# A two-layer decoder trunk on one core: more raw weight buffers, sums in smaller parts, sums of h on another queue, out projections by two row blocks

## The chip, the cores and the metric

One NeuronCore of a Trainium2 chip runs the program. Its engines work side by side: TensorE (PE; its weight loads are shown as PEld), VectorE (DVE), ScalarE (ACT), GpSimd (POOL) and SyncE (SP), which only issues transfers. Each engine runs its own instructions strictly in order; an instruction that waits holds all that stand behind it. Transfers are issued by SP, by ScalarE or by GpSimd, and all of them run on the same 16 DMA engines. The metric is the device time of one execution in microseconds, the median of three runs.

## The reference

Two decoder layers on x of shape (1, 512, 1024) in float32, each closed by a LayerNorm over `alpha * x + sublayer(x)`.

- The even (first) layer has one input projection of 1024 x 6144. Its columns feed chunkwise retention (8 heads with rotary q and k, a GroupNorm per head) and an RG-LRU branch (a causal convolution of width 4, block-diagonal gates, a scan). Both are multiplied by a SiLU gate path, concatenated, and mapped back by an output projection of 2048 x 1024.
- The odd (second) layer is differential attention: an input projection of 1024 x 8192 gives q and k for 16 maps of width 128, and v and the gate g of width 2048. A head subtracts lambda times its second softmax map from its first one, multiplies by v (width 256), normalises, and is gated by silu(g). An output projection of 2048 x 1024 follows.

```
q, k, v, g = split(x @ w_in)
w = softmax(q1 k1) - lam * softmax(q2 k2)
out = rmsnorm(w @ v) * subln_g * (1 - lambda_init) * silu(g)
y = out @ w_out;   x = layer_norm(alpha * x + y)
```

## The kernel before

**Products.** Every float32 matrix is held as a pair of rounded parts, high and low (`split`, L142: ScalarE makes the high part, VectorE the low one from the difference). A product is three matmuls (`mm3`, L151, shown as lines L152 to L154). S = 512 rows are four row blocks of 128; D = 1024 is eight tiles of 128.

**Weights.** They come in pieces of 128 x 1024 (512 KB), named w0 to w161 in the order of their use. `fetch` (L166) loads one piece into a raw buffer from SP (L174) and splits it into a pair (L148 and L149, or L145 and L146 where a scale goes in). The pool `wraw` has two raw buffers, `wsp` five split pairs. `take(ahead)` hands out the next piece and makes sure that `ahead` further ones have been fetched, as far as the program's order goes.

**Units.** `t_unit` uses a piece up in 24 matmuls (one head's 128 columns of q, k or a gate, for all 512 rows). `s_unit` makes 512 columns for four row blocks from four pieces. `out_unit` adds an output projection to the running sum y: with four pieces it goes through the row blocks one at a time, and for each through both 512-wide halves, first with pieces 0 and 1 and then with 2 and 3; its results lie in two PSUM banks of the pool `ps_pj` (four banks).

**`gates_values`** (L738) makes, for the second to fourth pair of heads of the second layer, the gate and v with seven block products instead of eight. For it sums of weight blocks and sums of blocks of h are needed:

- `weight_sums` (L382) makes 24 sums of weight blocks in HBM while the first layer runs: SP copies one block to the place t, and GpSimd issues a transfer that adds the second block to it. `SUM_GAP` = 18 is the number of steps between two sums.
- `act_sums` makes four sums of h once and stores them in HBM (sd). `load_sum` (L734) brings one of them into half of the tile sx (two transfers of 512 KB). `swap_in` loads two of them from SP. Inside `gates_values` two more calls stand between the products, issued by ScalarE; each overwrites what an earlier product has read, so it waits for TensorE.

sx and y lie in one place: y is put off to HBM (`store_y`, yd) ahead of `swap_in`, and fetched again at each out projection. A product of `gates_values` uses two pieces, 12 matmuls each.

**Order.** The order on TensorE and SP is the program's own. `Side` lays side work between the products: each `tick` (one step, after three matmuls) runs at most one due job. Jobs are the heads' retention, RG-LRU, the attention blocks (`attention`, L621: two score maps, Exp on ScalarE (L634), the combination on VectorE, transposes, the product with v), the LayerNorms and the sums. `need` runs a job until it is done. ScalarE, VectorE and GpSimd are put in order by the framework's scheduler at build time, by priorities and estimated times; after that their order is fixed.

**Memory.** The pools `es`, `qkp` and `two` belong to the first layer and are closed behind it (L612). `sp` (tiles for split scores), `gp` (five gates) and the small parameter tiles in `const` live through both layers.

Of the kernel before, what the change touches and what calls it, by code (L numbers as in the profile page):

```python
# [8 lines left out]
F32 = mybir.dt.float32  # L9
# [32 lines left out]
WARM_UP = 7  # L42
EARLY = 2

SUM_START, SUM_GAP = 40, 18


class Side:
# [49 lines left out]
def trunk(ctx: ExitStack, tc: tile.TileContext, a):  # L98
# [3 lines left out]
    def pool(name, bufs, stack=ctx, **kw):  # L102
        return stack.enter_context(tc.tile_pool(name=name, bufs=bufs, **kw))

    const = pool("const", 1)
    big = pool("big", 1)
    wraw = pool("wraw", 2)
    wsp = pool("wsp", 5)
    vp = pool("vp", 4)
    mixp = pool("mixp", 3)  # L110
    sp = pool("sp", 1)
    wk = pool("wk", 4)
    gp = pool("gp", 5)
# [16 lines left out]
    def bank(pl, tag, name):  # L130
        return pl.tile([P, 512], F32, tag=tag, name=name)

    def pair(pl, shape, tag, name, **kw):
        return tuple(pl.tile(shape, F32R, tag=tag + x, name=name + x, **kw) for x in "hl")

    def part(n, name):
        return pair(sp, [P, n], f"s{n}", name, bufs=2 if n == S else 1)

    def cut(t, *ix):
        return t[0][ix], t[1][ix]  # L140
# [25 lines left out]
    def fetch(parts=((0, D),)):  # L166
        if len(ready) < len(order):
            n = len(ready)
            src, scale = order[n]
            raw = wraw.tile([P, D], F32, tag="raw", name=f"w{n}_r")  # L170
            w = pair(extra.pop(n, wsp), [P, D], "w", f"w{n}")
            for lo, hi in parts:
                c = slice(lo, hi)
                nc.sync.dma_start(out=raw[:, c], in_=src[:, c])  # L174
                split(raw[:, c], cut(w, ALL, c), scale=scale)
                yield
            ready.append(w)
# [44 lines left out]
    def out_unit(mix, y, name, first, before=None, after=None, late=0):  # L222
        n = len(mix)
        w = [take(1 if n == 2 else 0) for _ in range(n)]
        y = y() if callable(y) else y
        for sb in range(SB):
            pss = [bank(ps_pj, "pj", f"{name}_ps{sb}{hf}") for hf in range(2)]
            steps = [(c, hf) for c in range(0, n, 2) for hf in range(2)]
            if late and sb == SB - 1:
                steps.sort(key=lambda t: t[1])  # L230
            for c, hf in steps:
                if before is not None and hf == 0:
                    before(c // 2, sb)
                for i in range(c, c + 2):
                    mm3(pss[hf], cut(mix[i], ALL, slice(sb * P, sb * P + P)), cut(w[i], ALL, slice(hf * HALF, hf * HALF + HALF)), i == 0, i == n - 1)
                    side.tick()
            for hf, ps in enumerate(pss):
# [11 lines left out]
            if after is not None:  # L249
                after(sb)  # L250

    ev = [("v", 0)]
    for p in range(3):
# [127 lines left out]

    def weight_sums():  # L382
        for dst, one, two in sums:
            nc.sync.dma_start(out=dst, in_=one)
            nc.gpsimd.dma_start(out=dst, in_=two, max_dma_last_dim=4 * D, accum_op=ALU.add)  # L385
            yield SUM_GAP


    phase = ctx.enter_context(ExitStack())
    es = pool("es", 10, phase)  # L390
    qkp = pool("qkp", 2, phase)
    two = pool("two", 2, phase)
    y = big.tile([P, SB, D], F32, tag="y", name="y")
    vecs = load("vecs", [P, 8, KT], a["vecs"])
# [4 lines left out]
    gn = load("gn", [P, 2, KT], a["gn"])  # L399
    gng = const.tile([P, KT], F32, tag="gng", name="gng")  # L400
# [4 lines left out]
    sin = load("sin", [P, S], a["sin"])  # L405


    sp4 = const.tile([P, KT], F32, tag="sp4", name="sp4")
    sa = const.tile([P, KT], F32, tag="sa", name="sa")
    sb_ = const.tile([P, KT], F32, tag="sb_", name="sb_")  # L410
    sc = const.tile([P, KT], F32, tag="sc", name="sc")
# [198 lines left out]


    phase.close()  # L612
    lq = load("lq", [P, 4, P], a["lq"].partition_broadcast(P), pl=wk, tag="wk")
    nc.vector.tensor_tensor(out=lq[:, 0:2], in0=lq[:, 0:2], in1=lq[:, 2:4], op=ALU.mult)
    ls = const.tile([P, 2], F32, tag="ls", name="ls")
# [115 lines left out]
        for n, t in enumerate(st):  # L731
            nc.sync.dma_start(out=sd[n], in_=t)

    def load_sum(n, k, queue=nc.scalar):  # L734
        for j in range(2):
            queue.dma_start(out=sx[:, k, :, 2 * j:2 * j + 2].bitcast(F32), in_=sd[n][:, :, 2 * j:2 * j + 2])

    def gates_values(i):  # L738
        def block(r, c):
            return lambda kt, n: cut(h, ALL, 4 * c + kt, slice((2 * r + n) * P, (2 * r + n) * P + P))  # L740

        def total(k):
            return lambda kt, n: tuple(sx[:, k, x, kt, n * P:n * P + P] for x in range(2))

        def product(ps, left, start):
            for j in range(2):
                w = take(3)
                for n in range(2):
# [48 lines left out]
        vt[i] = side.now + GV_VALUE  # L797
# [16 lines left out]
    def swap_in():  # L814
        nonlocal sx
        sx = big.tile([P, 2, 2, KT // 2, 2 * P], F32R, tag="y", name="sx")
        load_sum(1, 0, nc.sync)
        load_sum(2, 1, nc.sync)

    def qk_unit(n, name):  # L820
        r = rope(t_unit(h, name), n, name)
# [135 lines left out]
```

## Time and profile before

| | |
|---|---|
| runs | 973.29, 977.56, 976.13 us; median 976.13 us |
| the profiled execution | 977.99 us; span 976.2 us; mean granted clock 0.984 |
| TensorE | 926.3 us busy (95%), 4255 matmuls |
| weight loads of TensorE | 757.8 us (78%) |
| VectorE | 736.4 us (75%) |
| ScalarE | 501.9 us (51%) |
| GpSimd | 81.7 us (8%) |
| SP's transfers | 133.29 MB, 38.9% of the 16 DMA engines' span |
| GpSimd's transfers | 12.58 MB, 7.4% |
| ScalarE's transfers | 6.29 MB, 2.0% |

The span runs from the first to the last instruction. The first layer fills about the first 430 us, the second the rest. The names in the profile: w121h and w121l are the two parts of piece 121; `gv2a` and `gv2b` the PSUM banks of `gates_values` for the third pair of heads; `oo_ps` those of the second layer's out projections; e, wt, po and o belong to attention; t is a sum of weights and sx a sum of h. "PE gv2b L152 <- ACT w121h L148" says that TensorE stood idle before the product into gv2b until ScalarE had made w121h. The granted clock is the share of full speed that TensorE had.

### The profile page before, as it was taken

What the parts mean: (1) busy time and instruction counts of PE and PEld (TensorE: products, weight loads), DVE (VectorE), ACT (ScalarE), POOL (GpSimd) and SP (SyncE); (2) the same over time, 40 slices, a digit from 0 to 9 for tenths busy, and PEclk for the clock granted to TensorE, in tenths of its full rate; (3) what the DMA queues carried; (4) which work ended last, traced back from release to release, by engine and by line L of the source; (5) the groups of instructions that cost most, each with busy time, mean ns of one, the idle gap of its engine ahead of it and who ended that gap; (6) DMA issues with size and microseconds to landing.
All of it is one profiled execution on the core that took longest, in us unless ns stands there. A gap on an engine that the chain in (4) does not pass through costs nothing.

```text
span 976.2 us, 11727 instructions
## 1 busy us (share of the span) xinstructions
PE 926.3 (95%) x4255; PEld 757.8 (78%) x4255; DVE 736.4 (75%) x1221; ACT 501.9 (51%) x798; POOL 81.7 (8%) x142
## 2 busy tenths in 40 slices
PE   9999999979999899899999999899998999998996
PEld 7888878768887787688877887688776788777885
DVE  5788996857768887898588876569845579767777
ACT  4567876456374666433344476334564324665240
POOL 0000000100001000010001220100110100101022
PEclk9999999989999999999999999999998999999999
DMA  6895561953838352322862245553346263254602
GB/s 217 256 309 136 172 174 36 276 152 94 260 83 253 86 152 85 122 71 90 323 206 95 70 148 176 216 215 130 103 157 229 95 235 110 87 194 130 216 22 87
DMA packets 44794, 152.92 MB, mean 157 GB/s; under 512 B 5312, under 2 KB 5440, under 8 KB 43840
## 3 DMA queue, kind: packets, MB, share of 16 engines
q1 hardware_dynamic: 38016, 133.29, 38.9%
q0 software_dynamic: 3456, 12.58, 7.4%
q10 hardware_dynamic: 3264, 6.29, 2.0%
q8 instruction: 33, 0.54, 0.2%
q14 instruction: 25, 0.20, 0.1%
HBM read 139.57 MB, written 37.75 MB: 182 GB/s over the span
## 4 chain that ended last, share of the span: by engine, by line
PE 56%; DVE 17%; ACT 11%; DMA 9%; issue 4%; POOL 1%; SPq 0%; DVEq 0%; ACTq 0%; POOLq 0%
DMA w_r<-in_ev_w 4%; DMA w_r<-in_od_w 2%; PE oo_ps L153 2%; PE oo_ps L154 2%; PE oo_ps L152 2%; PE ev_ps L152 2%; PE ev_ps L153 2%; PE ev_ps L154 2%; DMA w_r<-t 2%; ACT e L634 2%; DMA w_r<-in_ev_wo 1%; PE xb_ps L152 1%; PE xb_ps L153 1%; PE xb_ps L154 1%; ACT L634 1%
## 5 line engine op out<-in xcount | busy, mean ns | idle before, releaser
L665 DVE SCALAR_TENSOR_TENSOR o<-po,ars,og 128x256 f32<-128x256 f32 x32 | 15.5, 484 | 38.3 <-POOL ars L342 32.2
L634 ACT ACTIVATE e<-as,nm 128x128 f32<-128x128 f32 (+3 forms) x64 | 33.2, 523 | 20.3 <-DVE nm L631 20.2
L641 POOL TENSOR_SCALAR zr<-z 128x1 f32<-128x1 f32 x32 | 16.8, 527 | 311.1 <-ACT e L634 311.1
L631 DVE CUSTOM_DVE_ANT_0 as<-as,mask 128x128 f32<-128x128 f32 (+3 forms) x64 | 30.3, 509 | 1.7 <-PE as L154 1.7
L385 POOL DMA_DIRECT2D t<-t x12 | 9.9, 825 | 207.6 <-DMA t<-in_od_w 189.3
L661 ACT ACTIVATE po<-po 128x256 f32<-128x256 f32 x32 | 11.9, 373 | 29.6 <-PE po L154 29.6
L341 POOL TENSOR_SCALAR rs_t<-ss,zr 128x1 f32<-128x1 f32 x32 | 14.5, 453 | 146.5 <-ACT po L661 141.5
L243 DVE TENSOR_TENSOR y<-oo_ps,y 128x512 f32<-128x512 f32 x24 | 16.3, 686 | 6.0 <-PE oo_ps L154 6.0
L385 POOL DMA_DIRECT2D t<-in_od_w x12 | 10.4, 863 | 121.7 <-DMA t<-in_od_w 121.7
L342 POOL TENSOR_TENSOR ars<-rs_t,nhalf 128x1 f32<-128x1 f32 x32 | 18.8, 589 | 2.7
L639 DVE RECIPROCAL zr<-z 128x1 f32<-128x1 f32 x32 | 5.2, 161 | 18.4 <-ACT e L634 18.0
L642 DVE SCALAR_TENSOR_TENSOR e<-e,zr,e 128x128 f32<-128x128 f32 (+3 forms) x32 | 17.6, 550 | 0.8
L504 DVE SCALAR_TENSOR_TENSOR xc<-xbp,vecs,xc 128x509 f32<-128x509 f32 (+2 forms) x24 | 17.9, 746 | 0.2
L646 PE MATMUL wt<-ident,e 128*128 128x128 f32 x80 | 14.2, 275 | 3.9 <-DVE e L642 3.9
L646 PEld LDWEIGHTS wt<-ident,e 128*128 128x128 f32 x80 | 10.0, 140 | 8.9 <-DVE e L642 4.2
L461 DVE TENSOR_TENSOR rsd<-rs,dec 128x512 f32<-128x512 f32 (+3 forms) x32 | 15.4, 485 | 1.7 <-PE rs L154 1.6
L634 ACT ACT_TABLE_LOAD x9 | 11.5, 1283 | 8.2 <-DVE nm L631 8.2
L670 PEld LDWEIGHTS po<-ident,o 128*128 128x128 f32 x64 | 8.4, 140 | 9.3 <-DVE o L665 6.1
L670 PE MATMUL po<-ident,o 128*128 128x128 f32 x64 | 12.6, 278 | 3.1 <-DVE o L665 2.9
L526 DVE SCALAR_TENSOR_TENSOR xc<-t,r 128x512 f32<-128x512 f32 x8 | 5.5, 692 | 12.1 <-ACT r L525 12.1
L634 ACT ACTIVATION_READ_ACCUMULATOR e<-as,nm 128x1 f32 x64 | 12.5, 196 | 0.0
L520 DVE TENSOR_TENSOR xbp<-xbp,xc 128x512 f32<-128x512 f32 x8 | 5.5, 690 | 9.0 <-ACT xbp L517 9.0
(2847 smaller groups left out, 3502.0 us busy)
## 6 DMA issues: line engine op xcount, KB each, us to landing
w_r<-in_od_w SPq DMA_DIRECT2D x58, 512.0 KB, 3.7
w_r<-in_ev_w SPq DMA_DIRECT2D x47, 512.0 KB, 3.9
t<-in_od_w SPq DMA_DIRECT2D x24, 512.0 KB, 6.0
w_r<-t SPq DMA_DIRECT2D x24, 512.0 KB, 3.3
w_r<-in_ev_wo SPq DMA_DIRECT2D x16, 512.0 KB, 5.1
w_r<-in_od_wo SPq DMA_DIRECT2D x16, 512.0 KB, 3.6
t<-in_od_w POOLq DMA_DIRECT2D x12, 512.0 KB, 6.3
t<-t POOLq DMA_DIRECT2D x12, 512.0 KB, 6.1
```

What stands on the lines that cost most here:

```text
L152: nc.tensor.matmul(out=out, lhsT=l[0], rhs=r[0], start=start, stop=False, **kw)
L153: nc.tensor.matmul(out=out, lhsT=l[0], rhs=r[1], start=False, stop=False, **kw)
L154: nc.tensor.matmul(out=out, lhsT=l[1], rhs=r[0], start=False, stop=stop, **kw)
L342: nc.gpsimd.tensor_tensor(out=out, in0=t, in1=nhalf[:, :1], op=ALU.pow)
L385: nc.gpsimd.dma_start(out=dst, in_=two, max_dma_last_dim=4 * D, accum_op=ALU.add)
L504: nc.vector.scalar_tensor_tensor(out=xc[:, sh:], in0=xb[:, :S - sh], scalar=conv_w(w, c), in1=xc[:, sh:], op0=ALU.mult, op1=ALU.add)
L631: nc.vector.tensor_tensor_reduce(out=ps[:, :n], in0=ps[:, :n], in1=mask[:, S - n:], scale=-QK_SCALE, scalar=3.0e38, op0=ALU.add, op1=ALU.m ...
L634: nc.scalar.activation(out=e, in_=ps[:, :n], func=AF.Exp, scale=-1.0, bias=nm, accum_out=z[:, mp:mp + 1])
L641: nc.gpsimd.tensor_scalar(out=zr[:, 1:2], in0=z[:, 0:1], scalar1=z[:, 0:1], scalar2=EPS, op0=ALU.mult, op1=ALU.mult)
L642: nc.vector.scalar_tensor_tensor(out=ee[0], in0=ee[1], scalar=zr[:, 0:1], in1=ee[0], op0=ALU.mult, op1=ALU.add)
L646: nc.tensor.transpose(out=pt[:, kb * P:kb * P + P], in_=ee[0][:, kb * P:kb * P + P], identity=ident)
L670: nc.tensor.transpose(out=pm[:, i * P:i * P + P], in_=o[:, i * P:i * P + P], identity=ident)
```

## The change

Four edits are made together.

1. **Raw buffers.** Behind the first layer a second pool of two raw buffers is opened; pieces then go through the two pools in pairs, so that four buffers serve in turn. Room comes from other pools: the tiles for split scores (`sp`) and the gates (`gp`) get a pool for each layer, in the second with one 512-wide pair instead of two and four gates instead of five, and the first layer's parameter tiles move into a pool that is closed with it.
2. **Weight sums.** Each sum is made in four parts of 32 rows (128 KB), a copy by SP and an addition by GpSimd for each, with four steps between two parts.
3. **Sums of h.** The two `load_sum` calls in `gates_values` are issued by SP. Each now stands inside the product behind the one that reads the old sum, between its two pieces.
4. **Out projections** with four pieces, and no LayerNorm that follows them row by row, go through two row blocks at a time: pieces 0 and 1 for both blocks and halves, then pieces 2 and 3. A group has four PSUM banks.

```diff
-SUM_START, SUM_GAP = 40, 18
+SUM_START, SUM_GAP, SUM_ROWS = 40, 4, 32
...
-    wraw = pool("wraw", 2)
+    raws = [pool("wraw", 2)]
...
-        return pair(sp, [P, n], f"s{n}", name, bufs=2 if n == S else 1)
+        return pair(sp, [P, n], f"s{n}", name, bufs=full if n == S else 1)
...
-            raw = wraw.tile([P, D], F32, tag="raw", name=f"w{n}_r")
+            raw = raws[n // 2 % len(raws)].tile([P, D], F32, tag="raw", name=f"w{n}_r")
...
-        for sb in range(SB):
-            pss = [bank(ps_pj, "pj", f"{name}_ps{sb}{hf}") for hf in range(2)]
-            steps = [(c, hf) for c in range(0, n, 2) for hf in range(2)]
-            if late and sb == SB - 1:
-                steps.sort(key=lambda t: t[1])
-            for c, hf in steps:
+        step = 2 if n == 4 and after is None else 1
+        for sbs in (range(i, i + step) for i in range(0, SB, step)):
+            pss = {(sb, hf): bank(ps_pj, "pj", f"{name}_ps{sb}{hf}") for sb in sbs for hf in range(2)}
+            steps = [(c, sb, hf) for c in range(0, n, 2) for sb in sbs for hf in range(2)]
+            if late and sbs[0] == SB - 1:
+                steps.sort(key=lambda t: t[2])
+            for c, sb, hf in steps:
...
         for dst, one, two in sums:
-            nc.sync.dma_start(out=dst, in_=one)
-            nc.gpsimd.dma_start(out=dst, in_=two, max_dma_last_dim=4 * D, accum_op=ALU.add)
-            yield SUM_GAP
+            for lo in range(0, P, SUM_ROWS):
+                r = slice(lo, lo + SUM_ROWS)
+                nc.sync.dma_start(out=dst[r], in_=one[r])
+                nc.gpsimd.dma_start(out=dst[r], in_=two[r], max_dma_last_dim=4 * D, accum_op=ALU.add)
+                yield SUM_GAP
...
     phase.close()
+    raws.append(pool("wraw2", 2))
+    sp, full = pool("sp2", 1), 1
+    gp = pool("gp2", 4)
...
-            queue.dma_start(out=sx[:, k, :, 2 * j:2 * j + 2].bitcast(F32), in_=sd[n][:, :, 2 * j:2 * j + 2])
+            nc.sync.dma_start(out=sx[:, k, :, 2 * j:2 * j + 2].bitcast(F32), in_=sd[n][:, :, 2 * j:2 * j + 2])
...
-        def product(ps, left, start):
+        def product(ps, left, start, then=()):
             for j in range(2):
+                if j and then:
+                    load_sum(*then)
                 w = take(3)
...
-        load_sum(0, 0)
-        product(two, total(1), True)
+        product(two, total(1), True, (0, 0))
         p7 = copies(two, "p7")
-        load_sum(3, 1)
-        product(one, total(0), False)
+        product(one, total(0), False, (3, 1))
```

More of the change, by code (lines that the diff above doesn't have):

```diff
@@ L110, in trunk @@
     mixp = pool("mixp", 3)
-    sp = pool("sp", 1)
     wk = pool("wk", 4)
-    gp = pool("gp", 5)
     small = pool("small", 4)
@@ L225, in out_unit @@
         y = y() if callable(y) else y
-        for sb in range(SB):
-            pss = [bank(ps_pj, "pj", f"{name}_ps{sb}{hf}") for hf in range(2)]
-            steps = [(c, hf) for c in range(0, n, 2) for hf in range(2)]
-            if late and sb == SB - 1:
-                steps.sort(key=lambda t: t[1])
-            for c, hf in steps:
+        step = 2 if n == 4 and after is None else 1
[5 more added lines that the diff above has]
+            for c, sb, hf in steps:
                 if before is not None and hf == 0:
                     before(c // 2, sb)
+                ps = pss[sb, hf]
                 for i in range(c, c + 2):
-                    mm3(pss[hf], cut(mix[i], ALL, slice(sb * P, sb * P + P)), cut(w[i], ALL, slice(hf * HALF, hf * HALF + HALF)), i == 0, i == n - 1)
+                    mm3(ps, cut(mix[i], ALL, slice(sb * P, sb * P + P)), cut(w[i], ALL, slice(hf * HALF, hf * HALF + HALF)), i == 0, i == n - 1)
                     side.tick()
-            for hf, ps in enumerate(pss):
+                if c < n - 2:
+                    continue
                 yy = y[:, sb, hf * HALF:hf * HALF + HALF]
@@ L248, in out_unit @@
                         stats[sb] = st
-            if after is not None:
-                after(sb)
+                if after is not None and hf:
+                    after(sb)
     ev = [("v", 0)]
@@ L391, in trunk @@
     qkp = pool("qkp", 2, phase)
+    sp, full = pool("sp", 1, phase), 2
+    gp = pool("gp", 5, phase)
+    evc = pool("evc", 1, phase)
     two = pool("two", 2, phase)
     y = big.tile([P, SB, D], F32, tag="y", name="y")
-    vecs = load("vecs", [P, 8, KT], a["vecs"])
+    vecs = load("vecs", [P, 8, KT], a["vecs"], evc)
     conv_w = lambda i, c: vecs[:, i, c:c + 1]
@@ L398, in trunk @@
     gbx = lambda c: vecs[:, 6, c:c + 1]
-    gn = load("gn", [P, 2, KT], a["gn"])
-    gng = const.tile([P, KT], F32, tag="gng", name="gng")
+    gn = load("gn", [P, 2, KT], a["gn"], evc)
+    gng = evc.tile([P, KT], F32, tag="gng", name="gng")
     nc.vector.tensor_scalar(out=gng, in0=gn[:, 0], scalar1=-0.5, scalar2=None, op0=ALU.mult)
@@ L405, in trunk @@
     sin = load("sin", [P, S], a["sin"])
[L408 to L411, printed above, removed]
+    sp4 = evc.tile([P, KT], F32, tag="sp4", name="sp4")
+    sa = evc.tile([P, KT], F32, tag="sa", name="sa")
+    sb_ = evc.tile([P, KT], F32, tag="sb_", name="sb_")
+    sc = evc.tile([P, KT], F32, tag="sc", name="sc")
     lam = vecs[:, 7]
@@ L732, in act_sums, with load_sum @@
             nc.sync.dma_start(out=sd[n], in_=t)
-    def load_sum(n, k, queue=nc.scalar):
+    def load_sum(n, k):
         for j in range(2):
-            queue.dma_start(out=sx[:, k, :, 2 * j:2 * j + 2].bitcast(F32), in_=sd[n][:, :, 2 * j:2 * j + 2])
+            nc.sync.dma_start(out=sx[:, k, :, 2 * j:2 * j + 2].bitcast(F32), in_=sd[n][:, :, 2 * j:2 * j + 2])
     def gates_values(i):
@@ L816, in swap_in @@
         sx = big.tile([P, 2, 2, KT // 2, 2 * P], F32R, tag="y", name="sx")
-        load_sum(1, 0, nc.sync)
-        load_sum(2, 1, nc.sync)
+        load_sum(1, 0)
+        load_sum(2, 1)
     def qk_unit(n, name):
```

## The prediction

> **What bounds the kernel now.** I read the page first, then the waits of TensorE, then a table of stretches, then the chain of waits around the worst of them. From the page (span; busy time by engine; the chain's shares):
>
> ```profile
> span 976.2 us, 11727 instructions
> PE 926.3 (95%) x4255; PEld 757.8 (78%) x4255; DVE 736.4 (75%) x1221; ACT 501.9 (51%) x798; POOL 81.7 (8%) x142
> PE 56%; DVE 17%; ACT 11%; DMA 9%; issue 4%; POOL 1%; SPq 0%; DVEq 0%; ACTq 0%; POOLq 0%
> ```
>
> TensorE is the bound, yet 44% of the chain is something else: there are places where it waits. The table of stretches shows them (length; busy time and count of each engine; granted clock, DMA share, GB/s). The first row is a stretch without any wait, as a measure.
>
> ```profile
> 640.00:660.00 20.00, 20.00 (x90) 16.54 (x89) 13.92 (x20) 5.59 (x7) 0.00 (x0) 1.00 0.66 237
> 505.00:520.00 15.00, 12.76 (x57) 10.49 (x56) 12.48 (x26) 8.92 (x18) 1.69 (x2) 0.89 0.45 146
> 598.00:602.00 4.00, 2.52 (x14) 1.82 (x13) 3.99 (x8) 3.37 (x5) 0.00 (x0) 1.00 0.08 31
> 611.00:620.00 9.00, 6.59 (x31) 4.67 (x31) 4.24 (x7) 1.99 (x4) 0.81 (x2) 1.00 0.97 386
> 728.00:738.00 10.00, 7.78 (x26) 5.74 (x25) 5.73 (x8) 5.72 (x7) 0.00 (x0) 0.83 0.59 210
> 743.00:760.00 17.00, 13.04 (x44) 9.22 (x44) 6.95 (x9) 4.69 (x8) 0.81 (x2) 0.80 0.65 244
> 867.00:880.00 13.00, 10.70 (x44) 7.75 (x43) 8.21 (x10) 7.86 (x10) 0.00 (x0) 1.00 0.49 166
> 886.00:907.00 21.00, 17.66 (x89) 13.75 (x88) 17.15 (x30) 10.42 (x19) 3.18 (x7) 1.00 0.38 125
> 190.00:210.00 20.00, 13.56 (x53) 10.24 (x53) 10.52 (x17) 7.68 (x13) 2.22 (x3) 0.83 0.77 207
> 312.00:326.00 14.00, 10.90 (x41) 8.14 (x40) 11.47 (x18) 8.54 (x13) 0.81 (x1) 0.88 0.36 85
> ```
>
> In the first row 90 products take 20 us, 0.222 us each. What a stretch loses I take as its length less TensorE's busy time, plus (1 - granted clock) times the length, for a busy TensorE at a lower clock does half the work:
>
> - second layer: 505: 2.24 + 1.65 = 3.9; 598: 1.5; 611: 2.4; 728: 2.22 + 1.70 = 3.9; 743: 3.96 + 3.40 = 7.4; 867: 2.3; 886: 3.3
> - first layer: 190: 6.44 + 3.40 = 9.8; 312: 3.10 + 1.68 = 4.8
>
> The clock's part is seen in single products on TensorE's timeline (start, time), behind the waits for w121:
>
> ```profile
> 735.73 0.63 PE L152 MATMUL gv2b<-w121h,hh 128*128 128x512 f32 x1
> 736.16 0.63 PE L153 MATMUL gv2b<-w121l,hh 128*128 128x512 f32 x1
> ```
>
> The starts are 0.43 us apart, where a product at speed takes 0.222. Who is waited for, from the waits of TensorE (total, times, longest):
>
> ```profile
> PE gv2b L152 <- ACT w121h L148: 1.5, 1, 1.5
> PE oo_ps L152 <- ACT w101h L145: 1.4, 1, 1.4
> PE oo_ps L153 <- DVE w127l L146: 1.2, 1, 1.2
> PE gv3b L153 <- DVE w147l L149: 0.8, 1, 0.8
> ```
>
> So 611 (w101), 728 (w121), 743 (w127) and 867 (w147) wait for weights that are not yet split. Why they are late stands in the chain of waits (start, time, what), here ahead of w101's wait, and one load from ahead of w121's:
>
> ```profile
> 590.81 4.96 DMA w_r<-in_od_w
> ...
> 596.76 1.23 ACT e L634 x4
> ...
> 601.88 4.76 DMA w_r<-in_od_wo
> ...
> 606.72 1.16 ACT w99h L145
> ...
> 607.90 1.30 DVE w99l L146
> ...
> 609.21 3.60 DMA w_r<-in_od_wo
> ...
> 723.91 7.14 DMA w_r<-t
> ```
>
> This is a ring through two raw buffers: w99 is loaded and split, and only then, 0.01 us behind the split's end at 609.20, does w101's load start, into the same buffer. One turn is 4.76 + 1.16 + 1.30 and some issue, 7.3 us for two weights (each buffer turns by itself), 3.7 us a weight. A product of `gates_values` uses a weight up in 12 matmuls, 12 x 0.222 = 2.7 us, so there the ring is the slower one; a `t_unit` takes 24, 5.3 us, and hides it. The same ring holds ScalarE: its Exp (L634) at 596.76 came only after the load of 590.81 had landed. ScalarE's timeline shows that at 508 too (in brackets the idle time):
>
> ```profile
> 508.26 1.05 ACT L148 CAST w80h<-w_r 128x1024 fp32r<-128x1024 f32 x1 [1.21 <-DMA w_r<-in_od_w]
> 509.33 1.28 ACT L634 ACT_TABLE_LOAD   x1
> ```
>
> **Four raw buffers (second layer).** A load then waits for the split four weights back. The ring gives four weights in 7.3 us, 1.8 us a weight, below the 2.7 us used. The five split pairs remain, but do not bind there: w99's split began 0.08 us after its landing (606.64), and w101's load left with the split's end, so the wait was for a raw buffer and not for a pair. I take the four stretches that name weights whole: 2.4 + 3.9 + 7.4 + 2.3 = 16.0, and the two in which ScalarE stood before a load, 3.9 + 1.5 = 5.4. That at 886 names no weight, ends in attention's own steps and stays. Together -21.4; from below, 886 goes as well (-24.7); from above, half of it returns because attention's steps, which the stalls covered, are next in line (-10.7).
>
> **Out projections, two row blocks.** Nothing is added: the same matmuls, with 24 instead of 12 (5.3 instead of 2.7 us) before the third weight is read, and w's first pair freed 24 matmuls before the end instead of 12. The wait for w127 lies in the 7.4 counted above; with the buffers alone part of it might stay, with both it goes. All four PSUM banks of the group are taken at once, but their evictions come while the second pair is multiplied. I put it at nothing of its own, -1 to +1.
>
> **Sums of h by SyncE.** Their issues, from the groups that name `sx` (ns min/median/max):
>
> ```profile
> L736 SPq DMA_DIRECT2D sx<-sd x12: 533/610/612, 486.6 to 787.3; - x12
> ```
>
> Twelve issues leave ScalarE, which is not the bound. On SP they bring a new wait: `load_sum` waits until TensorE has read the old sum, and behind it in SP's order stand all later weights. They do not stand close: `take(3)` has put the loads up to three weights ahead before it, so the weight behind it is used four weights after the product that it waits for, 4 x 2.66 = 10.7 us and attention's matmuls besides. By then two issues, the load and its split must be through. With the 7.14 us of the load at 723.91, which had two such transfers beside it, that is 2 x 0.61 + 7.14 + 1.16 + 1.30 = 10.8: with attention's matmuls it just fits. With the 3.7 us that loads of `in_od_w` take in the middle (the row is below) it has 3.5 us to spare. Six such places: 0 if they fit, some 2 us each (the 728 stretch halved) if they do not, 0 to +12. I take +3, near the lower end, since the nearest row just fits.
>
> **Sums of weights in parts of 128 KB.** Issues and landing, from the groups that name `t` (ns) and from the list of transfers (KB each, us to landing):
>
> ```profile
> L384 SPq DMA_DIRECT2D t<-in_od_w x24: 494/495/1434, 25.9 to 344.2; - x24
> L385 POOL DMA_DIRECT2D t<-in_od_w x12: 812/814/1161, 32.1 to 312.0; - x12
> w_r<-in_od_w SPq DMA_DIRECT2D x58, 512.0 KB, 3.7
> t<-in_od_w SPq DMA_DIRECT2D x24, 512.0 KB, 6.0
> ```
>
> 24 issues become 96 on each queue: 72 x 0.495 = +36 us of SP and 72 x 0.81 = +59 us of GpSimd, both in the first layer, where GpSimd does nothing else and SP mostly waits. Each accumulation waits on GpSimd for its part to land; behind it stand only later accumulations, first needed in the second layer. The bytes are the same, spread at 16 instead of 18 steps a sum. A weight that stood behind a whole 512 KB sum now stands behind 128 KB twice. At 190 the loads suffered from just that; I take back 3 of its 9.8, and give 1 for the issues: -2. Bounds: the stretches at 190 and 312 gone (-14.6), or as much again (+14.6).
> The Trainium skill ("DMA: Bandwidth & Descriptors", Rules for kernel authors) speaks against it: for bandwidth it wants at least 1 MiB a transfer and calls those under 64 KB mostly overhead; the same page (Anatomy of one DMA) puts some 2 us fixed on each. Were that served one after the other, 72 x 2 = 144 us more of it would lie on the queue (an estimate from the page); the trace differs: in the 611 stretch 386 GB/s are moved, 1.4 us for 512 KB, while each such load takes 3.6 to 4.8 us to land, so transfers overlap and only the issue remains. The rule's case is the slow rival below.
>
> **The rest.** Gates have four buffers instead of five, the 512-wide attention tile one instead of two, and the new pools lie where the first layer's temporaries were. The reader of the older buffer is an attention block that `need` has already put ahead in TensorE's order. 0, up to +3.3 (886 once more).
>
> **Sum.** The profiled execution took 977.99 us (its span 976.2 and 1.8 around it), 1.86 above the median 976.13 of the runs shown. 977.99 - 21.4 + 3 - 2 = 957.6; less the 1.86, for the median, 955.7: I say 956.
>
> **The rivals.**
> 1. *Attention's steps become the bound.* DVE is 75% busy and every weight still costs it 1.3 us; a faster TensorE reaches the softmax steps earlier and waits there. For it: the 3.3 us at 886. Against: at 640 TensorE runs full beside 70% DVE. Half of the gain: 956 + 10.7 = 967.
> 2. *The first layer gains too.* The late loads at 190 and 312 come from whole sums in the ring ahead of them. Then 14.6 instead of 2: 956 - 12.6 = 943.
> 3. *Slower: the parts hold up SP in the first layer*, which keeps two raw buffers. Some 48 weights are loaded while sums run, two parts before each, 2 x 0.495 = 1.0 us: up to +48 us if all lay on the path. It decides from the point where more than 42% of it does (20.4 of 48); with half, 956 + 2 + 24 = 982. For it: 190 to 210, where loads already are on the path. Against: a `t_unit` needs a weight each 5.3 us and the ring of two gives one each 3.7 us, so 1 us more is still hidden in most of the layer.
> 4. *The buffers don't act*: split pairs or the fixed order of ScalarE and DVE hold the splits where they were. Then only the parts count: 974. Against: the 0.01 us above.
>
> **How the numbers follow.** Forecast 0.54, its own range 949 to 966 (886 gone as well, the SP wait at 0 and the out projections at -1; or the SP wait at +12 and these at +1). Rival 1: 0.18; rival 2: 0.12; rival 3: 0.08; rival 4: 0.08. A difference under 0.5%, 4.9 us, can't be told from no change here. Faster by more: forecast, rivals 1 and 2, less a fifth of rival 1 that ends above 971.2: 0.80. Within: that fifth, rival 4 and a little of rival 3: 0.13. Slower: 0.07. The range 943 to 973 leaves out rival 3, most of 4 and half of 2.
>
> **What would show it.** In the profile after, waits of TensorE should no longer name w101, w121, w127 or w147, and the stretches of `gates_values` and the out projections in the second layer should have clock 1.00. SP's waits should show `load_sum` waiting for matmuls of about a weight's length. If those rows are gone and the time is not, rival 1 shows as more waits for `e`, `o` and `wt`. I am wrong if TensorE waits for the first weight behind a `load_sum`, or if the first layer, up to the first LayerNorm, is longer than before.

## The result, and the profile after

The changed kernel takes 946.43 us (median of four runs, 943.23 to 947.8), the kernel before 976.85 (973.29 to 978.6): a ratio of 0.9688, with a 95% interval of 0.9651 to 0.9726. It is 30.4 us faster, where 20.1 were forecast (976.13 to 956). The two profiled executions lie 34.8 us apart: the changed kernel's (943.23) is the fastest of its four, and the one before (977.99) lies 1.1 us above its median. The gains by stage below are read from these two and add up to the 34.8.

The page of the changed kernel (span; busy time by engine; the chain's shares):

```profile
span 941.4 us, 11931 instructions
...
PE 912.3 (97%) x4255; PEld 752.8 (80%) x4255; DVE 735.0 (78%) x1221; ACT 502.3 (53%) x798; POOL 139.7 (15%) x214
...
PE 62%; DVE 19%; ACT 8%; issue 4%; DMA 3%; POOL 2%; SPq 0%; DVEq 0%; ACTq 0%; POOLq 0%
```

TensorE's share of the chain went from 56 to 62%, that of transfers from 9 to 3%. The mean granted clock rose from 0.984 to 0.994, and with it TensorE's busy time fell, by 14 us for the same 4255 products.

Where the time went is read from the groups of products that open a stage: the last two numbers ahead of the semicolon are the first and the last start. First the kernel before, then the changed one.

```profile
L152 PE MATMUL ov_ps<-w64h,hh x8: 387/389/477, 430.0 to 449.3; 128*128 128x512 f32 x8
L152 PE MATMUL gv1a<-w84h,hh x4: 387/392/483, 558.0 to 562.0; 128*128 128x512 f32 x4
L152 PE MATMUL gv2a<-w110h,hh x4: 389/389/478, 689.8 to 692.3; 128*128 128x512 f32 x4
L152 PE MATMUL gv3a<-w136h,hh x4: 389/389/478, 828.8 to 831.2; 128*128 128x512 f32 x4
```

```profile
L150 PE MATMUL ov_ps<-w64h,hh x8: 387/389/475, 418.6 to 437.6; 128*128 128x512 f32 x8
L150 PE MATMUL gv1a<-w84h,hh x4: 387/392/476, 543.0 to 546.9; 128*128 128x512 f32 x4
L150 PE MATMUL gv2a<-w110h,hh x4: 389/389/476, 671.1 to 673.5; 128*128 128x512 f32 x4
L150 PE MATMUL gv3a<-w136h,hh x4: 389/389/476, 798.4 to 800.9; 128*128 128x512 f32 x4
```

The second layer opens with the product into `ov_ps`. So:

| from | to | before, us | after, us | gain | predicted losses there that should go |
|---|---|---|---|---|---|
| start | ov_ps | 430.0 | 418.6 | 11.4 | 2 |
| ov_ps | gv1a | 128.0 | 124.4 | 3.6 | 505: 3.9 |
| gv1a | gv2a | 131.8 | 128.1 | 3.7 | 598 and 611: 1.5 + 2.4 = 3.9 |
| gv2a | gv3a | 139.0 | 127.3 | 11.7 | 728 and 743: 3.9 + 7.4 = 11.3 |
| gv3a | end of span | 147.4 | 143.0 | 4.4 | 867: 2.3 (886, another 3.3, was to stay) |

The second layer gained 23.4 us and the first one 11.4, of which 2 had been forecast. From here on "first layer" is the time to the first product into `ov_ps`, and "second layer" the rest of the span. Five programs, the changed kernel and four of the experiments (a_raw2, a_actsx, a_raw2_actsx, a_raw3), have no difference in the first layer's code; it took 418.3 to 422.3 us in their profiles, so a difference of up to 4 us there tells nothing. Five likewise have no difference in the second layer's code (the changed kernel, a_sum512, a_sumburst, a_sum64, a_ahead): 522.8 to 525.0 us, of which 143.0 to 144.7 lie behind gv3a. So 2 us in the second layer tell nothing either, and the gain behind gv3a is 2.7 to 4.4 us.

The waits of TensorE in the changed kernel (total, times, longest):

```profile
PE po L680 <- DVE o L675: 4.2, 6, 1.3
PE pi L150 <- DVE rsd L468: 2.4, 1, 2.4
PE rv L485 <- ACT rq7h L146: 2.3, 1, 2.3
...
PE po L150 <- DVE om6l L147: 2.1, 2, 1.7
...
PE ev_ps L150 <- ACT w0h L146: 0.6, 1, 0.6
```

The only piece of weights that is named is w0, the first. What is left in the second layer are attention's last steps (o, om6). From the table of stretches (length; busy time and count of each engine; granted clock, DMA share, GB/s), the places that answer to 611, 728 and 743 of before:

```profile
590.00:632.00 42.00, 41.02 (x200) 33.80 (x199) 22.94 (x37) 15.19 (x29) 4.11 (x9) 1.00 0.51 187
705.00:720.00 15.00, 15.00 (x69) 12.36 (x68) 13.21 (x21) 11.83 (x18) 0.87 (x1) 1.00 0.63 233
720.00:740.00 20.00, 19.03 (x95) 15.47 (x94) 10.23 (x20) 6.62 (x16) 2.72 (x7) 1.00 0.61 238
```

TensorE lacks 1.0 us in the first and in the last and nothing in the second, at clock 1.00. SyncE does wait at the loads of sums (L746), among others here:

```profile
SPq L746 <- PE gv2a L152: 11.2, 1, 11.2
SPq L746 <- PE gv3a L152: 11.2, 1, 11.2
```

That is about the time of four weights (10.7 us), where the prediction had named one weight's as the sign.

Last the list of transfers (KB each, us to landing):

```profile
w_r<-in_od_w SPq DMA_DIRECT2D x58, 512.0 KB, 5.6
w_r<-in_ev_w SPq DMA_DIRECT2D x47, 512.0 KB, 4.4
t<-in_od_w SPq DMA_DIRECT2D x96, 128.0 KB, 4.8
```

A weight of the second layer lands in 5.6 us, where before it took 3.7. It is slower and no longer waited for: it leaves up to four pieces ahead.

### The profile page after: what moved, and what is told of

Read it like the earlier page. It is cut to its first block, busy times and chain, and to the rows that moved or that the text cites. A ratio compares the mean times of both kernels' runs of the same rounds, so it can differ in the third digit from the quotient of the medians.

```text
span 941.4 us, 11931 instructions
## 1 busy us (share of the span) xinstructions
PE 912.3 (97%) x4255; PEld 752.8 (80%) x4255; DVE 735.0 (78%) x1221; ACT 502.3 (53%) x798; POOL 139.7 (15%) x214
## 4 chain that ended last, share of the span: by engine, by line
PE 62%; DVE 19%; ACT 8%; issue 4%; DMA 3%; POOL 2%; SPq 0%; DVEq 0%; ACTq 0%; POOLq 0%
PE oo_ps L150 2%; PE oo_ps L151 2%; PE oo_ps L152 2%; DMA w_r<-in_ev_w 2%; PE ev_ps L151 1%; PE ev_ps L152 1%; PE ev_ps L150 1%; PE out_ps L150 1%; PE out_ps L152 1%; PE out_ps L151 1%; DMA w_r<-in_ev_wo 1%; PE xb_ps L150 1%; PE xb_ps L152 1%; PE xb_ps L151 1%; ACT e L644 1%
## 5 line engine op out<-in xcount | busy, mean ns | idle before, releaser
L389 POOL DMA_DIRECT2D t<-in_od_w x48 | 38.5, 944 | 118.1 <-DMA t<-in_od_w 117.5
L389 POOL DMA_DIRECT2D t<-t x48 | 38.2, 897 | 111.9 <-DMA t<-in_od_w 102.6
L343 POOL TENSOR_SCALAR rs_t<-bmv 128x1 f32<-128x1 f32 x6 | 2.8, 468 | 122.5 <-DVE bmv L354 122.5
L527 DVE TENSOR_TENSOR xbp<-xbp,xc 128x512 f32<-128x512 f32 x8 | 5.5, 691 | 11.4 <-ACT xbp L524 11.4
L146 ACT CAST hh<-ht 128x512 fp32r<-128x512 f32 x8 | 4.7, 587 | 16.3 <-PE ht L608 16.3
## 6 DMA issues: line engine op xcount, KB each, us to landing
t<-in_od_w SPq DMA_DIRECT2D x96, 128.0 KB, 4.8
t<-in_od_w POOLq DMA_DIRECT2D x48, 128.0 KB, 5.2
```

What stands on the lines that cost most here:

```text
L343: nc.gpsimd.tensor_scalar(out=t, in0=var, scalar1=scale, scalar2=eps, op0=ALU.mult, op1=ALU.add)
L389: nc.gpsimd.dma_start(out=dst[r], in_=two[r], max_dma_last_dim=4 * D, accum_op=ALU.add)
```

## The experiments

The theory going in had two parts: in the second layer the ring of two raw buffers was the whole loss and the other two edits add little; in the first layer the sums in small parts let the weights through. All lengths are from the profiles, one for each kernel; the ratios are each against the kernel before on the same chip. For reference: before 430.0 + 546.2 us, after 418.6 + 522.8 (first and second layer).

### Two raw buffers again (a_raw2)

```diff
-    raws.append(pool("wraw2", 2))
```

> The changed kernel with two raw buffers in the second layer as before; the other three edits stay. Theory (the ring of two raw buffers held the second layer): TensorE again waits for weights by name there, the second layer is 10 to 20 us longer than in the changed kernel, the first layer is the same within 1 us; about 960 us. Rival (the second layer gained because ScalarE no longer issues the sums of h, or because of the out projections' new order): under 4 us longer, about 948 us, with no weight among TensorE's waits.

Measured: 952.01 us, ratio 0.9763 (0.9728 to 0.9798); first layer 419.4, second 532.4, 9.6 us longer (7.4 against the longest of the five with an unchanged second layer). But TensorE's waits name no weight of the second layer; they grew at attention:

```profile
PE po L150 <- DVE om6l L147: 3.5, 2, 2.2
...
PE po L150 <- DVE om2l L147: 2.4, 2, 2.2
```

The chain of waits ahead of such a place (start, time, what) shows why:

```profile
587.29 4.94 DMA w_r<-in_od_wo
...
592.32 1.16 ACT w99h L143
...
593.50 1.29 DVE w99l L144
...
594.81 3.67 DMA w_r<-in_od_wo
...
598.56 1.15 ACT w101h L143
599.71 0.40 ACT po L670 x2
...
601.83 0.49 DVE o L674
```

It is the ring of before, turn by turn: load, high part, low part, and the next load 0.02 us behind it. But now it is ScalarE that stands before w101, with attention's `po` behind it in its fixed order; TensorE waits for `o` instead of for a weight. The stall kept its cause and changed its name.

The 9.6 us are not all that the ring cost before. With two raw buffers the other edits and the moved pools still take the second layer from 546.2 to 532.4, 13.8 us, while four buffers alone take off 22.5 (b_raw4, below). The two remedies overlap: what the buffers are worth depends on what stands beside them. The stage from gv2a to gv3a shows it best. It takes 139.0 us before, 128.0 in b_raw4, and 127.6 here with two buffers: its loss is gone by either way.

### Two raw buffers, and the out projections one row block at a time (a_raw2_oneblock)

```diff
-        step = 2 if n == 4 and after is None else 1
+        step = 1
-    raws.append(pool("wraw2", 2))
```

> The changed kernel with two raw buffers and with out projections one row block at a time; sums in parts and sums of h by SyncE stay. Theory (with two raw buffers it is the two row blocks that keep TensorE from waiting for the third and fourth weight): waits for w101, w125 or w127 return, the second layer is 4 to 10 us longer than the 532 us that it took with two raw buffers; about 958 us. Rival (moving the sums of h to SyncE was what took these waits away): within 2 us, about 952 us.

Measured: 952.17 us, ratio 0.9761 (0.9705 to 0.9817); second layer 532.3, as with two row blocks. The waits for weights are back in the list:

```profile
PE oo_ps L150 <- ACT w127h L143: 1.3, 1, 1.3
PE oo_ps L150 <- ACT w101h L143: 1.2, 1, 1.2
```

So two row blocks do take away the waits that name w101 and w127, and it is worth nothing here: the second layer is as long, and the waits are at attention instead. Names in the list of waits are no measure of a cause.

### Out projections one row block at a time, with four raw buffers (a_oneblock)

```diff
-        step = 2 if n == 4 and after is None else 1
+        step = 1
```

> The changed kernel with the out projections one row block at a time. Theory (four raw buffers alone bring the third and fourth weight in time): within 2 us, about 947 us, no weight among TensorE's waits. Rival (the third weight is still late, since its split pair is freed too late): w101, w127 and w157 or their neighbours stand among the waits, 4 to 9 us longer in the second layer, 950 to 955 us.

Measured: 944.41 us, ratio 0.9684 (0.9644 to 0.9723); second layer 523.0 against 522.8. The edit has no effect of its own that these runs show.

### The sums of h issued by ScalarE, with four and with two raw buffers (a_actsx, a_raw2_actsx)

```diff
...
-        product(two, total(1), True, (0, 0))
+        load_sum(0, 0, nc.scalar)
+        product(two, total(1), True)
...
-        product(one, total(0), False, (3, 1))
+        load_sum(3, 1, nc.scalar)
+        product(one, total(0), False)
```

The second kernel also lacks the pool `wraw2`.

> The changed kernel with the two sums of h inside the products issued by ScalarE again, at their old places. Theory (with four raw buffers loads are far enough ahead, so it does not matter who issues them): within 2 us of the changed kernel, about 946 us. Rival (a waiting issue holds ScalarE, and with it attention and the splits): 4 to 10 us longer, in the three stretches of the value and gate products; 950 to 956 us.

> The changed kernel with two raw buffers and with the two sums of h issued by ScalarE; sums in parts and two row blocks stay. Theory (with two raw buffers, SyncE's issue of the sums of h is what keeps w121 and w147 in time): waits for w121 and w147 return, the second layer is 4 to 8 us longer than the 532 us with two raw buffers; about 957 us. Rival (these two waits were ended by the loads' other order alone, or by the two row blocks): within 2 us, about 952 us.

Measured, with four buffers: 946.3 us, ratio 0.9711 (0.9677 to 0.9744), second layer 524.8, 2.0 us longer, which is within the spread. With two: 960.75 us, ratio 0.9848 (0.9791 to 0.9905), second layer 539.3, which is 6.9 longer than with two buffers and SyncE. There weights are waited for again, among them one of `gates_values`:

```profile
PE gv3b L150 <- ACT w147h L146: 1.0, 1, 1.0
```

Issuing the sums from SyncE is worth 6.9 us where the ring is short, 6.4 of it from gv2a to gv3a (134.0 against 127.6), and nothing clear of the spread where it has four places. So half of the 13.8 us above is this edit; the other 6.9 us (546.2 to 539.3) came with the moved pools or the two row blocks, and no run separates these. SyncE's own wait at the sums never cost anything that these runs show.

### Three raw buffers (a_raw3)

```diff
-            raw = raws[n // 2 % len(raws)].tile(...)
+            raw = raws[n % 3 // 2 if len(raws) > 1 else 0].tile(...)
...
-    raws.append(pool("wraw2", 2))
+    raws.append(pool("wraw2", 1))
```

> The changed kernel with three raw buffers in the second layer. Theory (a ring of three gives a weight every 7.3 / 3 = 2.4 us, less than the 2.7 us that a product takes): second layer 522 to 526 us, about 946 us. Rival (the sums of h on SyncE's queue need the fourth one as a reserve): second layer 527 to 531 us, attention waits as with two; about 951 us.

Measured: 948.23 us, ratio 0.9715 (0.9678 to 0.9752); second layer 525.8, 3.0 more than with four and 6.6 less than with two. Only 1.8 of the 3.0 are clear of the spread: they lie from ov_ps to gv1a (126.2 us, against 124.2 to 124.5 in the five profiles of one code). The third buffer brings at least two thirds of the gain over two.

### The raw buffers and pools alone, and the parts of 128 KB alone (b_raw4, b_sum128)

Both start from the kernel before. The first gets the second pool and the moved pools (the core of it below) and keeps whole sums, ScalarE's issues and one row block. The second gets the sums in parts and nothing else.

```diff
+    raws.append(pool("wraw2", 2))
+    sp, full = pool("sp2", 1), 1
+    gp = pool("gp2", 4)
```

```diff
-SUM_START, SUM_GAP = 40, 18
+SUM_START, SUM_GAP, SUM_ROWS = 40, 4, 32
...
-            nc.sync.dma_start(out=dst, in_=one)
-            nc.gpsimd.dma_start(out=dst, in_=two, max_dma_last_dim=4 * D, accum_op=ALU.add)
-            yield SUM_GAP
+            for lo in range(0, P, SUM_ROWS):
+                r = slice(lo, lo + SUM_ROWS)
+                nc.sync.dma_start(out=dst[r], in_=one[r])
+                nc.gpsimd.dma_start(out=dst[r], in_=two[r], max_dma_last_dim=4 * D, accum_op=ALU.add)
+                yield SUM_GAP
```

> The kernel before with four raw buffers in the second layer alone, and the pools that make room for them (whole 512 KB sums, sums of h by ScalarE, out projections one row block at a time). Theory (the ring of raw buffers alone holds the second layer, and the edits to the out projections and to the sums of h are not needed beside it): the second layer takes 522 to 526 us, as in the changed kernel, the first 430 to 433; about 956 us. Rival (the other two edits share the gain): second layer 530 to 538 us, about 964 us, with weights among TensorE's waits.

> The kernel before with the sums in parts of 128 KB alone. Theory (the first layer's gain comes from the parts, the second layer's from the rest): first layer 418 to 422 us, second 545 to 547; about 966 us. Rival (the parts act only together with the pools or the out projections): first layer over 426 us, about 972 us.

Measured:

| kernel | median, us | ratio (95%) | first layer | second layer |
|---|---|---|---|---|
| b_raw4 | 956.73 | 0.9811 (0.975 to 0.9871) | 429.3 | 523.7 |
| b_sum128 | 965.76 | 0.9893 (0.982 to 0.9965) | 417.9 | 545.6 |

The buffers, with the pools that make room for them, give 22.5 of the second layer's 23.4 us by themselves; from stage to stage 3.6, 4.2, 11.0 and 3.7. The parts alone give 12.2 in the first layer, all of its 11.4 within the spread. 22.5 + 12.2 is 34.7, and the whole change gave 34.8 by its span (976.2 to 941.4): the two parts add up, each in its own layer. The runs' ratios agree: 0.9811 x 0.9893 = 0.9706, within the interval of the whole change.

### Whole sums again (a_sum512)

```diff
-SUM_START, SUM_GAP, SUM_ROWS = 40, 4, 32
+SUM_START, SUM_GAP, SUM_ROWS = 40, 18, 128
```

> The changed kernel with whole 512 KB sums, 18 steps apart, as before. Theory (the first layer's 11.4 us came from the smaller parts): the first layer is 8 to 12 us longer again, above all ahead of the second value unit, the second layer is the same; about 956 us. Rival (the first layer gained through the out projections' order, or through another fixed order on ScalarE and DVE): under 3 us, about 948 us.

Measured: 956.67 us, ratio 0.9803 (0.9768 to 0.9838); first layer 432.0 (13.3 longer), second 522.9. The stretch from 180 to 220 us in before, a_sum512, b_raw4, the changed kernel and b_sum128, a row each:

```profile
180.00:220.00 40.00, 33.56 (x142) 26.77 (x141) 24.96 (x38) 18.55 (x28) 3.31 (x4) 0.91 0.72 203
```

```profile
180.00:220.00 40.00, 34.61 (x147) 28.21 (x146) 24.82 (x38) 18.41 (x26) 4.13 (x5) 0.91 0.76 215
```

```profile
180.00:220.00 40.00, 35.65 (x147) 28.16 (x146) 26.60 (x42) 20.59 (x30) 3.29 (x4) 0.91 0.70 200
```

```profile
180.00:220.00 40.00, 38.81 (x177) 32.09 (x176) 28.25 (x45) 24.50 (x33) 11.76 (x15) 1.00 0.72 183
```

```profile
180.00:220.00 40.00, 38.22 (x173) 31.31 (x172) 28.03 (x43) 24.46 (x34) 11.81 (x15) 1.00 0.69 184
```

By the prediction's measure (length less busy time, plus the clock's part) the three with whole sums lose 10.0, 9.0 and 8.0 us here, and the two with parts 1.2 and 1.8. This is the larger piece of the first layer's gain. My reason for it, weights that land late behind whole sums, is not what the transfers show. Piece for piece, w30 to w35 took 3.7, 4.3, 7.7, 5.5, 8.8 and 9.9 us to land before and 5.0, 6.5, 7.1, 6.7, 6.8 and 8.6 after, 6.7 and 6.8 in the mean. Three landed sooner and three later. The one that matters most below, w34, landed 2.0 us sooner (KB, us to landing; before, then after):

```profile
w_r<-in_ev_w SPq DMA_DIRECT2D x1, 512.0 KB, 8.8
```

```profile
w_r<-in_ev_w SPq DMA_DIRECT2D x1, 512.0 KB, 6.8
```

So 2 to 3 us at this place can be w34's load itself (it took 9.3 in a_sum512, 7.0 in b_raw4, 6.2 in b_sum128); the six together landed no sooner. What differs besides is ScalarE's timeline (start, time, idle time ahead and what ended it). First a_sum512, then the changed kernel:

```profile
203.06 1.04 ACT L146 CAST w34h<-w_r 128x1024 fp32r<-128x1024 f32 x1 [5.86 <-DMA w_r<-in_ev_w]
204.01 0.51 ACT L146 CAST r31h<-rsd 128x384 fp32r<-128x384 f32 x1
```

```profile
192.24 1.05 ACT L146 CAST w33h<-w_r 128x1024 fp32r<-128x1024 f32 x1
195.05 0.51 ACT L146 CAST r31h<-rsd 128x384 fp32r<-128x384 f32 x1 [1.76 <-DVE rsd L468]
...
208.11 1.03 ACT L146 CAST w34h<-w_r 128x1024 fp32r<-128x1024 f32 x1
```

With whole sums the split of w34 stands ahead of r31h, a step of head 3's retention, and is itself held for 5.86 us by w34's load. TensorE then waits for r31h, as in the kernel before (4.3 us there); from a_sum512's waits of TensorE:

```profile
PE ro L150 <- ACT r31h L146: 4.5, 1, 4.5
```

With parts r31h, r32h and r33h come first, and w34 is split at 208, 8 us after it has landed. The order on ScalarE is made at build time, from estimated times. All three kernels with whole sums have w34h ahead of r31h; the changed kernel, a_sumburst and b_sum128 have it behind. In b_raw4 that split waits for 0.98 us only, but the splits of w31 to w33 ahead of it wait for 4.44, 2.13 and 2.41 us on ScalarE, and the stretch loses 8.0 us all the same; w33h stands ahead of head 3's first step, r30h, in all three kernels with whole sums and behind it in the other three.

That the order is different and holds up those steps is shown by the rows; how many of the 8.8 us it accounts for is not. That the scheduler's estimate of the transfers is why it differs is argued: no run kept the sums and changed the order alone.

### Four parts in one step (a_sumburst)

```diff
-SUM_START, SUM_GAP, SUM_ROWS = 40, 4, 32
+SUM_START, SUM_GAP, SUM_ROWS = 40, 16, 32
...
-                yield SUM_GAP
+            yield SUM_GAP
```

> The changed kernel with the four parts of a sum issued in one step and 16 steps between two sums: parts of 128 KB and the same rate, but in bursts. Theory (a load is late because 512 KB of a sum stand ahead of it, so spreading is what helps): the first layer is 428 to 432 us again, about 956 us. Rival (the size of a part helps, because the addition can begin when 128 KB have landed and a queue changes over to the loads after each part): first layer 418 to 422 us, about 946 us.

Measured: 944.06 us, ratio 0.9656 (0.962 to 0.9691); first layer 417.8, second 524.5. Four parts right behind each other are as good as four parts spread over 16 steps. The spreading, on which my theory of a clear ring rested, does nothing; the size of the part does (the sums also stand 16 steps apart here and 18 in a_sum512, which no run changed alone). This fits the order on ScalarE (w33h waits 0.52 us for its load, w34h for none and stands behind r33h) and not late landings.

### Parts of 64 KB (a_sum64)

```diff
-SUM_START, SUM_GAP, SUM_ROWS = 40, 4, 32
+SUM_START, SUM_GAP, SUM_ROWS = 40, 2, 16
```

> The changed kernel with parts of 64 KB (16 rows), two steps apart: 192 copies and 192 additions. Theory (spreading is what helps, issues are hidden): first layer within 2 us of 419, about 946 us. Rival (each further transfer costs SP 0.5 us and GpSimd 0.9 us, and small transfers are slow): first layer 424 to 440 us, 952 us or more.

Measured: 1036.71 us, ratio 1.0608 (1.0564 to 1.0651); first layer 512.7, that is 94 us longer, second 525.0. The rival had it slower, with a first layer of 424 to 440 us; neither foresaw this size. TensorE's longest waits name weights of the first layer:

```profile
PE gr_ps L150 <- ACT w43h L146: 8.3, 1, 8.3
...
PE gr_ps L150 <- ACT w34h L146: 5.6, 1, 5.6
```

The transfers are not slow (KB each, us to landing):

```profile
w_r<-in_ev_w SPq DMA_DIRECT2D x47, 512.0 KB, 4.3
t<-in_od_w SPq DMA_DIRECT2D x192, 64.0 KB, 3.5
```

GpSimd's issues of the additions (ns min/median/max):

```profile
L389 POOL DMA_DIRECT2D t<-in_od_w x96: 761/1348/3523, 30.3 to 385.8; - x96
```

Weights land in 4.3 us, as in the changed kernel (4.4). ScalarE's timeline ahead of the wait for w34:

```profile
278.31 0.62 ACT L146 CAST lrum2h<-xc 128x512 fp32r<-128x512 f32 x1 [4.63 <-DVE xc L542]
278.92 0.62 ACT L146 CAST ev13h<-vc 128x512 fp32r<-128x512 f32 x1
279.44 1.04 ACT L146 CAST w34h<-w_r 128x1024 fp32r<-128x1024 f32 x1
```

No transfer stands in the brackets of w34h: it comes after a block of RG-LRU and retention steps (lrum2h, ev13h) that ScalarE and VectorE work off in one piece, and waits for its turn. The splits of w25 (206.88) and w43 (352.72) likewise come right behind a step of the retention, without a wait for their loads. A reason lies in the program: `tick` runs at most one due job a step, and with two steps between the parts of a sum every second step goes to a sum; the heads and the RG-LRU fall behind until `need` runs them all at once. This is argued from the code and the chain; no run separated it from the 96 further issues on each queue, and at 94 us it stays the largest effect here without a proof.

### Two weights fetched ahead of the last steps of the first layer (a_ahead)

```diff
+    for _ in range(2):
+        list(fetch())
```

It stands ahead of the small loads before the first layer's last out projection; these loads otherwise stand in SP's order ahead of the last weights.

> The changed kernel with the next two weights (w60, w61) fetched ahead of the LayerNorm's parameters, whose transfers wait on SP for a tile of the first layer. Theory (these two loads were late because they stood behind that wait, and held ScalarE and so the last head's retention): the waits for rq7 at 382 us go, the first layer is 4 to 6 us shorter, about 941 us. Rival (the last head's retention is late by itself): within 1.5 us of the changed kernel, about 946 us.

Measured: 943.0 us, ratio 0.9647 (0.9618 to 0.9676); first layer 416.7, second 524.4. The wait for rq7h (2.3 us) is gone and a new one of 2.2 us for w63l stands at the same place in the layer:

```profile
PE eo_ps L151 <- DVE w63l L147: 2.2, 1, 2.2
```

By the medians it is 3.4 us faster than the changed kernel, but the intervals of the ratios overlap, and the first layer lies just below the 418.3 to 422.3 of its like. It is the fastest version run; that it beats the changed kernel is not settled, and the 4 to 6 us that were expected did not come.

## Why the prediction was right, and where it was wrong

- **Four raw buffers, -21.4: right, in mechanism and in size.** Alone they gave 22.5 (b_raw4). The table of stages shows it place by place: 3.6 for 3.9, 3.7 for 3.9, 11.7 for 11.3. Behind gv3a 2.7 to 4.4 came for the 2.3 that were taken; whether a part of the loss at 886, which I had left to attention, was the ring as well is not settled. The measure (idle time, plus half speed while the granted clock is low) held to within half a microsecond in the first three stages of the whole change. What the sum did not see is that the buffers are not the only cure: with two raw buffers the other edits and the moved pools take off 13.8 us, 6.9 of them by moving the sums' issues off ScalarE, which the prediction had put at no gain because ScalarE "is not the bound".
- **The reading "names a weight" against "ends in attention" was too fine.** a_raw2 loses 9.6 us to the ring without a single wait that names a weight of the second layer. Where ScalarE splits weights and serves attention in one fixed order, a late load shows up under either name. Taking the stretches at 505 and 598 into the sum was right; leaving out 886 by its name alone was not a sound reason.
- **Out projections, 0 ± 1: right.** 0.2 us with four buffers, 0.1 with two.
- **Sums of h on SyncE, +3 (0 to +12): mis-sized.** SyncE does wait, 11.2 us at gv2a and at gv3a, but no weight behind it is waited for; putting the issues back on ScalarE brings nothing back (2.0 us longer, within the spread), and with two raw buffers it costs 6.9. The case with room to spare was the true one. The term leaned on a load of 7.14 us; behind the second sum at gv2a in the changed kernel, w122's load took 5.4 us, its split began at 708.7, and TensorE first used it at 714.8. (By the prediction's own terms the 3.5 us to spare are 3.3, and the row that it shows for these issues is that of the loads which SyncE made already.)
- **Sums in parts of 128 KB, -2 (-14.6 to +14.6): the size was wrong, and the mechanism.** It is -12.2 alone (b_sum128) and +13.3 when taken back (a_sum512), near the lower bound. Of the places 190 was right: the loss from 180 to 220 us fell from 10.0 to 1.2, where 3 had been taken back; at 312 little changed (300 to 316 us of the changed kernel still loses 4.2). The step that failed is the sentence that the loads at 190 suffered from whole sums ahead of them in the queue: w30 to w35 land no sooner behind smaller parts (mean 6.8 against 6.7 us), though w34 among them by 2 to 3 us. What the rows show is that ScalarE's fixed order had the split of a weight in flight ahead of retention steps, which had to wait with it. I read how long w34's load took and not what stood behind its split.
- **The rivals.** The forecast was made of the second layer's gain with +3 - 2, and rival 2 had the first layer gain 14.6. What came is the forecast's second layer without the +3, together with most of rival 2's first layer. The measured 946.43 lies below the forecast's own 949 to 966; rival 2's 943 was nearest, and that is luck in part, for its mechanism, late loads, does not show in w30 to w35 taken together, and in w34 by 2 to 3 us. Rival 1 (attention as the bound) did not come: TensorE works 97% of the span. Rival 4 (buffers that don't act) fell with b_raw4. Rival 3 (parts that hold up SP) did not come at 128 KB. (With the 2 us that it adds back, it decides from 38% of the 48 us on and not from 42%.) At 64 KB the kernel is indeed slower, by 60 us, but not by that rival's mechanism: TensorE waits for splits whose loads have landed.
- **The rule against the change.** The Trainium skill ("DMA: Bandwidth & Descriptors", Rules for kernel authors) wants transfers of at least 1 MiB for bandwidth and calls those under 64 KB mostly overhead. Here the rule and the trace part at 128 KB: 144 further transfers go with a first layer that is 11 to 13 us shorter. These sums are needed only in the second layer, so nothing waits for their bandwidth. A part of 128 KB lands in 4.8 us and one of 64 KB in 3.5, against 6.0 for a whole copy: a small transfer is far from proportionally quicker, which goes the rule's way.

## What to carry to other kernels

Before giving a wait for a transfer to the transfer, look at the order of the engine that consumes it: a small instruction that waits for a load holds everything behind it. Count a shared cause, such as a ring of buffers, by runs and not by the names in the list of waits, among which its stalls move; and count it both ways, added alone and taken out alone. Here these gave 22.5 and 9.6 us, because the other edits cure a part of the same loss. Where a scheduler fixes an order at build time, a change in one place can reorder another, so measure each edit by itself in the layer in which it acts.

## What the runs showed of the hardware that was not expected

- The loads of the second layer's weights take longer to land with four buffers (median 5.6 us against 3.7), and the kernel is faster all the same. That more of them are under way at a time is the likely reason; no run tests it.
- The landing of a transfer from HBM to HBM shrinks far less than its size: 512, 128 and 64 KB took 6.0, 4.8 and 3.5 us in the median, beside the other loads. GpSimd's issue of an addition took 0.81 us with 24 of 512 KB and 1.35 with 192 of 64 KB; why is not shown.
- Short waits cost twice. By the prediction's measure, of the 10.0 us lost from 180 to 220 in the kernel before, 3.6 are the granted clock (0.91 over 40 us), though TensorE's idle time there, 6.4 us, lay in pieces of which the longest was 4.3.
